# The last rows of a layer's second FFN in two parts of half their length, their output issued from two DMA queues

## The chip, the cores and the metric

The kernel is one program on all 8 cores of one Trainium2 chip. The metric is device time in microseconds (us), taken from the slowest core. Most executions agree within 0.3%; some fall in a slower state, in which the cores of one die or of both run at a lower granted clock. Those executions (one of before with 1,452 us, for example) are left out of every ratio and reading here; where a run had one, it still counts in the median that is quoted.

Some cores matter more than others. The program has two variants: even cores (0, 2, 4, 6) and odd cores (1, 3, 5, 7) cut their rows differently. Before the change the even cores are about 4 to 5 us slower than their odd neighbours, so they set the time.

Most of what follows happens in the last 35 us. Since this stretch begins some microseconds earlier or later from core to core and from run to run, I give times in this tail as **+x**: us after the start of the last eviction of a 512-column tile by VectorE. That instruction comes just before the part of the program that the change touches, and lies at 1,286 to 1,291 us on the even cores. The page of a profile and the views of a core have times from the start of the core's span instead.

## The reference, cut to what matters

One layer of a streaming encoder: half-step FFN, mixing by attention and convolution, second half-step FFN, final normalisation.

```python
def rmsnorm(x, g):
    x32 = x.astype(jnp.float32)
    r = x32 * lax.rsqrt(jnp.mean(x32 * x32, axis=-1, keepdims=True) + EPS)
    return (r * g.astype(jnp.float32)).astype(x.dtype)

def swiglu(h, w_gate, w_up, w_down):
    return (jax.nn.silu(h @ w_gate) * (h @ w_up)) @ w_down

# ... first FFN, attention, convolution ...
        x = x + 0.5 * swiglu(rmsnorm(x, ffn2_norm[l]), ffn2_gate[l], ffn2_up[l], ffn2_down[l])
    return rmsnorm(x, final_norm)          # (cut)
```

The input has 4 x 4096 rows of 1024 features; `D_FF` is 2816. So each core has about 2,048 rows, which it works through in two groups.

## The kernel before

Data lie transposed: features on the partitions, in 8 tiles of 128 features (`kc`), rows along the free axis. The second group of an even core is a block of 512 rows and a block of 512 rows whose last pass is done in two parts of 256; an odd core ends with blocks of 512, 384 and 256 rows.

```python
PLANS = ((((512, False), (384, False), (256, False)),
          ((512, False), (512, False, (256, 256)))),       # even cores: two groups
         (((512, True), (512, False), (256, False)),
          ((512, False), (384, False), (256, False))))     # odd cores
```

In the last pass of the second FFN (`fi == 1`, `hf == 1`), TensorE makes one tile of 128 features of one part at a time; VectorE evicts it from PSUM (the memory that TensorE writes to) and adds it to `xres`; ScalarE squares it, GpSimd sums the squares.

```python
fine = blocks if gi == 0 else blocks[:-1] + g.parts[blocks[-1]]
order = [(dg, s, dm2) for s in fine for dg in range(4) for dm2 in range(2)]
# ...
for dg, s, dm2 in order:
    b = fb_take()                                   # a PSUM bank, of four
    for fl in range(nf):
        mm(b, 0, wv[:, fl, dm2 * 128:(dm2 + 1) * 128], AT[:, fl, c0:c0 + n], n, ...)
    rk, xi = ... (keys("x", g, dm, s), xo)
    dve(... out=xo, in0=bk, scalar=0.5, in1=xi ..., n, (("ps", b),) + rk, (xk,))     # L1048
    square(stats[s], g, dm, s)                      # ScalarE: square; GpSimd: add
    if dm == 7:
        S.add(0, norm_fin(stats[s], g, s, 3))       # a task, started when its inputs are there
```

`norm_fin` sums over the partitions by matmul, makes 1/rms with Ln and Exp on ScalarE, then normalises the 8 tiles on VectorE and issues the output. The last part goes out in pieces of 2 tiles, everything else in one piece of 8:

```python
    for kc in range(8):
        xk, xin = ... (keys("x", g, kc, s), xsl(g, kc, s))
        dve(... out=dst, in0=xin, scalar=gcol, in1=rt ..., xk + (("rstd", rr), "cs"), (wk,))   # L823
        if idx == 3:
            w = 2 if gi == 1 and s == g.fine[-1] else 8
            if kc % w == w - 1:
                # ... dst, src: tiles i*w to (i+1)*w of the part
                P.dma("sp", lambda h, dst=dst, src=src: h.dma_start(out=dst, in_=src), ...)    # L835
```

Who waits for whom is worked out from names ("keys") of the data. A part reads with its own key **and the key of its whole block**, and a write waits for every reader of any key that overlaps:

```python
def keys(kind, g, kc, s):
    r = g.par[s]
    return tuple((kind, g.gi, kc, x) for x in ([s, r] if r != s else ...))

def _toks(self, e, reads, writes):
    # ...
    for k in writes:
        for k2 in self.overlap.get(k, ()):
            # ...
            for t in self.readers.get(k2, {}).values():   # waits for readers of overlapping keys
                if t[2] != e or e != "pe":
                    yield t
```

So ScalarE's square of a tile of the last rows is put down as a reader of that tile of the whole block. When VectorE later normalises the same tile of the *first* rows of the block, it waits for this square, though they touch different columns.

The softmax here doesn't subtract the row's maximum and nothing guards it: scores larger than these inputs give would overflow.

## Time and profile before

| | before |
|---|---|
| time, median of 3 runs | 1325.45 us (1325.04 to 1452.33, the last slow) |
| spans of the even cores | 1321.5 to 1323.3 us |
| spans of the odd cores | 1317.3 to 1318.3 us |
| TensorE busy on core 6 | 98% |
| even cores: last matmul of the last pass | +17.9 |
| VectorE's last instruction | +25.8 |
| last landing of output | +30.2 to +30.9 |
| end of the span | +33.9 to +34.9 |

From the page (core 6, the slowest): busy times, and the shares of the chain of waits that ended last.

```profile
PE 1292.1 (98%) x8666; PEld 740.4 (56%) x8666; DVE 487.1 (37%) x899; ACT 407.0 (31%) x727; POOL 229.0 (17%) x266
...
PE 92%; DVE 3%; DMA 2%; issue 1%; ACT 1%; SPq 0%; DVEq 0%; POOL 0%; ACTq 0%; POOLq 0%
```

TensorE (PE) is busy all the time, up to the tail. A change of the tail alone can win or lose only microseconds of 1,325.

Busy time by stretches of core 6, for TensorE (its matmuls, then its weight loads), VectorE, ScalarE and GpSimd; the last two columns are the share of the core's 16 DMA engines that is busy, and what they move in GB/s.

```profile
1300.00:1304.00 4.00, 4.00 (x39) 3.47 (x38) 4.00 (x9) 1.83 (x5) 1.36 (x2) 1.00 0.00 0
1304.00:1308.00 4.00, 2.34 (x22) 1.86 (x19) 4.00 (x10) 1.58 (x4) 2.77 (x4) 1.00 0.47 197
1308.00:1312.00 4.00, 0.66 (x3) 0.29 (x3) 3.56 (x9) 1.22 (x3) 0.33 (x1) 0.76 0.89 361
1312.00:1316.00 4.00, 0.00 (x0) 0.00 (x0) 2.21 (x6) 0.00 (x0) 0.00 (x0) 0.50 1.04 344
1316.00:1320.00 4.00, 0.00 (x0) 0.00 (x0) 0.00 (x0) 0.00 (x0) 0.00 (x0) 0.50 0.45 153
```

And its issues of output in this time (KB each, us from issue to landing):

```profile
yout<-xres SPq DMA_DIRECT2D x1, 2048.0 KB, 7.1
yout<-xres SPq DMA_DIRECT2D x1, 1024.0 KB, 6.3
yout<-xres SPq DMA_DIRECT2D x4, 256.0 KB, 4.9
```

2 MB of the first block of 512 rows are issued at +17.1, 1 MB of the first 256 rows at +22.15, four pieces of 256 KB from +23.5 on. From 1308 to nearly 1318 the DMA engines are full or nearly so (0.89 up to 1312, 1.04 after it; a share over 1 comes from how the view counts packets and means full): the output is what ends last.

### The profile page before, as it was taken

Reading aid. Unit: us, or ns where it says so; the run is one execution under the profiler, and the core shown is the slowest. Engines: PE = TensorE matmul, PEld = TensorE weight load, DVE = VectorE, ACT = ScalarE, POOL = GpSimd, SP = SyncE. Lnnn points to the kernel's source line nnn. Section 1 sums busy time; section 2 is a strip of 40 time slices with the busy share of each in tenths; the row PEclk is TensorE's granted clock in tenths of the full one; section 3 lists DMA queues with packets and bytes.
Section 4 is the critical chain, followed back from the end, with each engine's and each line's share of the span. In section 5 each row is a group of like instructions: output and inputs, shape, how many; then the busy total and the mean of one; then the engine's idle time right before and its main releaser. Section 6 shows DMA issues by size and latency. Waiting matters only on the chain.

```text
span 1323.3 us, 23324 instructions; the slowest of 8 cores (1317.3 to 1323.3 us)
## 1 busy us (share of the span) xinstructions
PE 1292.1 (98%) x8666; PEld 740.4 (56%) x8666; DVE 487.1 (37%) x899; ACT 407.0 (31%) x727; POOL 229.0 (17%) x266
## 2 busy tenths in 40 slices
PE   7999999999999999999999999999999999999995
PEld 3655655566665666665564444446566664444444
DVE  4522222263745522222266222125455362222125
ACT  3411011242666421001236110114338661101123
POOL 2263000341003320000161000014120220000022
PEclk9999999999999999999999999999999999999998
DMA  8795226244930753243445844342784125433503
GB/s 187 164 217 116 49 47 120 42 127 142 193 70 2 188 91 72 53 76 53 73 52 101 218 80 82 66 76 49 171 208 103 34 39 111 75 65 64 112 0 130
DMA packets 33923, 129.55 MB, mean 98 GB/s; under 512 B 2832, under 2 KB 13200, under 8 KB 26896
## 3 DMA queue, kind: packets, MB, share of 16 engines
q0 software_dynamic: 18752, 97.33, 38.9%
q1 hardware_dynamic: 15056, 30.68, 6.8%
q8 instruction: 73, 1.20, 0.4%
q14 instruction: 42, 0.34, 0.1%
HBM read 193.54 MB, written 18.68 MB: 160 GB/s over the span
## 4 chain that ended last, share of the span: by engine, by line
PE 92%; DVE 3%; DMA 2%; issue 1%; ACT 1%; SPq 0%; DVEq 0%; POOL 0%; ACTq 0%; POOLq 0%
PE psA L561 53%; PE ps L561 39%; DVE hT L823 1%; DMA gscr_1<-dreg 1%; DMA ring<-wgu 1%; DVE xres L1048 1%; DVE xres L823 0%; DMA dreg<-gscr_1 0%; ACT L569 0%; DMA xres<-xin 0%; ACT rstd L574 0%; SPq L1673 0%; DVE xres L1556 0%; ACT pb L574 0%; POOL ssb L771 0%
## 5 line engine op out<-in xcount | busy, mean ns | idle before, releaser
L561 PE MATMUL psA<-hT,ring 128*128 128x512 bf16 (+2 forms) x3792 | 691.4, 344 | 1.7 <-DVE dreg L1139 1.0
L561 PEld LDWEIGHTS psA<-hT,ring 128*128 128x128 bf16 x3792 | 370.6, 98 | 316.1 <-issue 3.6
L574 ACT ACTIVATE dreg<-psA 128x512 f32<-128x512 f32 (+3 forms) x279 | 162.3, 587 | 688.1 <-PE psA L561 678.6
L561 PE MATMUL ps<-at,ring 128*128 128x512 bf16 (+2 forms) x1920 | 326.6, 332 | 0.0
L1014 DVE TENSOR_TENSOR at<-psA,dreg 128x512 bf16<-128x512 f32 (+2 forms) x213 | 130.1, 612 | 450.7 <-PE psA L561 427.3
L561 PEld LDWEIGHTS ps<-at,ring 128*128 128x128 bf16 x1920 | 187.6, 98 | 137.2
L1048 DVE SCALAR_TENSOR_TENSOR xres<-ps,xres 128x512 f32<-128x512 f32 (+2 forms) x160 | 88.5, 556 | 168.0 <-PE ps L561 168.0
L766 POOL TENSOR_TENSOR ssum<-ssum,sq 128x512 f32<-128x512 f32 (+2 forms) x102 | 103.2, 1012 | 169.4 <-ACT sq L574 165.6
L668 POOL DMA_DIRECT2D ring<-wgu x47 | 25.6, 546 | 522.9 <-PE ps L561 261.0
L561 PE MATMUL ps<-dreg,ring 128*128 128x256 bf16 (+4 forms) x704 | 85.7, 274 | 2.1 <-DMA dreg<-gscr_1 1.5
L574 ACT ACTIVATE sq<-xres 128x256 bf16<-128x256 f32 (+2 forms) x108 | 55.3, 519 | 99.8 <-DVE xres L1048 66.7
L823 DVE SCALAR_TENSOR_TENSOR hT<-xres,cs_sb,rstd 128x256 bf16<-128x256 f32 (+2 forms) x120 | 70.4, 644 | 12.4 <-ACT rstd L574 12.4
L561 PEld LDWEIGHTS ps<-dreg,ring 128*128 128x128 bf16 x704 | 55.2, 98 | 23.1 <-issue 4.4
L561 PE MATMUL ps<-hT,ring 128*128 128x512 bf16 (+2 forms) x352 | 63.4, 336 | 0.0
L561 PEld LDWEIGHTS ps<-hT,ring 128*128 128x128 bf16 x352 | 33.6, 98 | 25.5 <-issue 0.4
L569 ACT ACT_TABLE_LOAD x36 | 46.2, 1283 | 0.6
L574 ACT ACTIVATE pb<-psA 128x1024 bf16<-128x1024 f32 (+2 forms) x42 | 37.7, 915 | 8.1 <-PE psA L561 7.9
L1556 DVE TENSOR_TENSOR xres<-ps,xres 128x256 f32<-128x256 f32 (+2 forms) x48 | 24.9, 531 | 37.2 <-PE ps L561 37.1
L1576 POOL TENSOR_TENSOR dreg<-pb 128x2560 bf16<-128x2560 bf16 x8 | 35.8, 4502 | 0.7 <-DMA cwscr<-dreg 0.7
L668 POOL DMA_DIRECT2D ring<-wdA x16 | 8.6, 537 | 135.7 <-PE psA L561 135.3
L561 PE MATMUL ps<-at,hT 128*128 128x512 bf16 x136 | 30.8, 379 | 0.0
L561 PE MATMUL psA<-cb_sb 64*128 64x64 bf16 (+3 forms) x456 | 27.8, 223 | 0.0
(93 smaller groups left out, 588.5 us busy)
## 6 DMA issues: line engine op xcount, KB each, us to landing
ring<-wgu POOLq DMA_DIRECT2D x41, 1024.0 KB, 8.4
ring<-wdA POOLq DMA_DIRECT2D x16, 768.0 KB, 8.6
ring<-wdB POOLq DMA_DIRECT2D x16, 640.0 KB, 7.9
ring<-cwscr POOLq DMA_DIRECT2D x16, 640.0 KB, 9.7
cwscr<-dreg SPq DMA_DIRECT2D x8, 640.0 KB, 6.1
ring<-wab POOLq DMA_DIRECT2D x8, 512.0 KB, 8.2
ring<-wout POOLq DMA_DIRECT2D x4, 1024.0 KB, 14.7
dreg<-xin SPq DMA_DIRECT2D x2, 2048.0 KB, 21.9
```

Of the source, the lines that this page charges most:

```text
L561: P.op("pe", lambda h: h.matmul(o, lhsT=lhsT, rhs=rhs, start=start, stop=stop, skip_group_check=True), (max(n / 2400.0 + 0.0025, 0.03) if ...
L569: P.op("act", lambda h: h.activation(out=cs[0:1, CS_N + i:CS_N + i + 1], in_=onesS[0:1, 0:1], func=func), 1.5, ("cb1",), ())
L574: P.op("act", lambda h: h.activation(out=out, in_=in_, func=func, **kw), 0.12 + n / 1200.0 + (0.09 * sum(isinstance(v, bass.AP) for v in k ...
L668: P.dma("pool", lambda h, dst=dst, src=src: h.dma_start(out=dst, in_=src), wtok(p, i), (256 if p.reads else 512) * w, reads=p.reads, after ...
L766: pool(lambda h: h.tensor_tensor(out=ss, in0=ss, in1=sqt, op=ALU.add), n, (sk, ("sq", i)), (sk,))
L823: dve(lambda h, dst=dst, xin=xin, gcol=gcol: h.scalar_tensor_tensor(out=dst, in0=xin, scalar=gcol, in1=rt, op0=ALU.mult, op1=ALU.mult), n, ...
L1014: dve(lambda h: h.tensor_tensor(out=at, in0=ub, in1=tt, op=ALU.mult), n, (("ps", bU), ("tmpF", ti)), (("AT", gi, fl, s),))
L1048: dve(lambda h, xo=xo, xi=xi, bk=bk: h.scalar_tensor_tensor(out=xo, in0=bk, scalar=0.5, in1=xi, op0=ALU.mult, op1=ALU.add), n, (("ps", b), ...
L1556: dve(lambda h, xo=xo, bk=bk: h.tensor_tensor(out=xo, in0=bk, in1=xo, op=ALU.add), n, (("ps", b),) + rk, (("x", gi, dm, s),))
L1576: P.op("pool", lambda h, o_=o_, i0=i0: h.tensor_tensor(out=o_, in0=i0, in1=i1, op=ALU.mult), 4.5, ("cmp", "ic", "cb"), (("cwb", i % 2),))
```

## The change

The intent: after the last matmul there remains a serial chain for the last rows (eviction, square, sum over features, Ln, Exp, normalise, output). With 128 rows in it instead of 256 it should be shorter. The last pass of the second group takes its last part as two halves (`g.last`); the last half goes out in two pieces of 4 tiles, the second of them issued by ScalarE (`"act"`) rather than SyncE (`"sp"`). The other three stages keep the old parts.

```diff
+        self.last, self.of = self.fine[:], {}
+        if gi:
+            p = self.last.pop()
+            for i in range(2):
+                f, n = len(self.n), self.n[p] // 2
+                ...
+                self.par[f], self.of[f] = self.par[p], p
+                self.last.append(f)
 ...
             def keys(kind, g, kc, s):
                 r = g.par[s]
+                if s in g.of:
+                    return tuple((kind, g.gi, kc, x) for x in dict.fromkeys((s, g.of[s], r)))
 ...
-                        w = 2 if gi == 1 and s == g.fine[-1] else 8
+                        w = 4 if gi == 1 and s == g.last[-1] else 8
 ...
-                            P.dma("sp", lambda h, dst=dst, src=src: h.dma_start(out=dst, in_=src),
+                            P.dma("act" if w == 4 and i else "sp", lambda h, dst=dst, src=src: h.dma_start(out=dst, in_=src),
 ...
-                        fine = blocks if gi == 0 else blocks[:-1] + g.parts[blocks[-1]]
+                        fine = blocks if gi == 0 else blocks[:-1] + (g.parts[blocks[-1]] if fi == 0 else [
+                            x for x in g.last if g.par[x] == blocks[-1]])
```

More of the change, by code (lines that the diff above doesn't have):

```diff
@@ L278, in __init__ @@
         self.fine = [f for i in self.main for f in self.parts[i]]
+        self.last, self.of = self.fine[:], {}
[3 more added lines that the diff above has]
+                f, n = len(self.n), self.n[p] // 2
+                self.n.append(n)
+                self.halo.append(False)
+                self.off.append(self.off[p] + i * n)
+                self.par[f], self.of[f] = self.par[p], p
+                self.last.append(f)
         self.M = self.T - self.H
@@ L422, in make @@
                         P.reg(("k", gi, j, s), "at", 2 * (MMAX * j + m0), 2 * (MMAX * j + m0 + n))
-                for s in g.fine:
+                for s in g.fine + list(g.of):
                     m0, n, w = g.off[s] - g.H, g.n[s], g.n[g.par[s]]
@@ L430, in make @@
                             P.reg(("h", gi, kc, s), "h%d" % kc, c0, c0 + n)
+                    if s in g.of:
+                        continue
                     for j in range(4):
@@ L700, in keys @@
                 r = g.par[s]
+                if s in g.of:
+                    return tuple((kind, g.gi, kc, x) for x in dict.fromkeys((s, g.of[s], r)))
                 return tuple((kind, g.gi, kc, x) for x in ([s, r] if r != s else [s] + [f for f in g.parts[s] if f != s]))
@@ L1779, in _unpack @@
         g = Group(i, blocks)
-        for n in (g.n[s] for s in g.fine):
+        for n in (g.n[s] for s in g.last):
             out.append(yo[:, 8 * o0:8 * (o0 + n)].reshape(128, 8, n).transpose(2, 1, 0).reshape(n, D)[_order(n)])
```

## The prediction

> **What bounds the kernel.** The page of the slowest core (6) gives TensorE 98% of 1323.3 us, and the chain of waits is 92% PE. So nothing before the last pass can change; the change only touches the tail. The even cores decide: 1321.5 to 1323.3 us against 1317.3 to 1318.3 for the odd ones (list of cores).
>
> **The tail of core 6 (timeline and DMA packets).** The last rows' 80 matmuls of 256 columns end at 1306.3. From 1297.8 to 1310.5 VectorE has almost no gap: it evicts PSUM (0.33 us apart at 256 columns) and normalises the block of 512 (about 0.8 us per piece) and the first 256 rows (0.40 us per piece). So the last eviction starts only at 1308.5, 2.2 us after its matmuls. Square, sum, Ln and Exp follow until 1310.9, then eight pieces of 0.40 us until 1314.2. The output of the first 256 rows is issued at 1310.6; from its first packet, 1311.6, to about 1318 the DMA engines are at a share of 1.0, moving 2,048 packets of 1 KB at 49 ns each over 16 engines. SP's issues for the last rows take up to 1.44 us instead of 0.37, and the last landing is at 1319.3. Then PE's closing branch takes 3.6 us on even cores only.
>
> **What the change does, costed from the trace.**
> - PE: 160 matmuls of 128 columns for 80 of 256. Start to start is 109 ns at 256 and 56 ns at 128 columns (conv matmuls, which also load weights each time): +0.2 us, plus one more set of three summing matmuls. [...]
> - VectorE: evictions at 512, 384 and 256 columns give an estimate of 0.20 us apart at 128. 16 of those replace 8 of 0.33: +0.6 us. Normalising 16 pieces of an estimated 0.26 replaces 8 of 0.40: +1.0 us in all, but only 2.1 instead of 3.2 us of it comes after the last Exp.
> - The last serial chain (eviction, square, sum, Ln, Exp) is about 0.4 us shorter.
> - DMA: the last 1 MB becomes 2,048 packets of 512 B. This trace has 512-byte packets at 27 to 29 ns, so 3.5 us instead of 3.1: +0.4 us.
> - Issue: ScalarE issues the last half, so SP's slow issues no longer delay it. But the DMA engines were saturated. [...] share 1.0 here agrees that the engines, not the issuing, limit.
>
> **On the critical path.** VectorE is full until about 1310.5, so the shorter chain after the last matmul mostly doesn't show: I expect its end at about 1315 (was 1314.2). The 256 rows' output is issued no earlier (1310.5 to 1311.3), and after it the same 2 MB has to drain, 0.4 us slower. Last landing about 1319.8 (was 1319.3); odd cores up to 1 us later, hidden. Net +0.3 us, between -2.5 and +3.
>
> **Predicted:** 1325.8 us, range 1322.5 to 1328.5. Faster by over 2%: 0.01; within 2%: 0.97; slower: 0.02.
>
> **Right or wrong by:** matmuls of 128 columns 56 ns apart; 512-byte packets about 28 ns; the output of the first 256 rows issued within 0.7 us of 1310.6 from the same point; DMA share about 1.0 until the end; last VectorE piece near 1315; last landing near 1319.8.
>
> **What would make it wrong:** the new program order lets VectorE finish the first 256 rows earlier, so that the DMA drains sooner (up to 2 us gained); PSUM banks, refilled twice as fast, stall PE behind VectorE (1 to 2 us lost); the second queue costs set-up; two of three runs in the slow state.

Two estimates give no source. For 0.26 us per piece, the trace of before (core 6) has instructions of 0.74 us at 512 columns and 0.47 at 256, so 128 columns less take about 0.13 off the 0.40. For the 0.4 us by which the last chain is to be shorter, none is given.

## More of the kernel before

The timeline of VectorE (DVE) on core 2: start, us that the group takes, line, operation, shapes, count, and in brackets idle time before it and what ended that.

```profile
1303.74 0.74 DVE L1048 SCALAR_TENSOR_TENSOR xres<-ps,xres 128x256 f32<-128x256 f32 x2
1304.41 0.87 DVE L823 SCALAR_TENSOR_TENSOR xres<-xres,cs_sb,rstd 128x256 f32<-128x256 f32 x2
1305.20 0.41 DVE L1048 SCALAR_TENSOR_TENSOR xres<-ps,xres 128x256 f32<-128x256 f32 x1
1305.53 1.43 DVE L823 SCALAR_TENSOR_TENSOR xres<-xres,cs_sb,rstd 128x256 f32<-128x256 f32 x2
1306.88 0.41 DVE L1048 SCALAR_TENSOR_TENSOR xres<-ps,xres 128x256 f32<-128x256 f32 x1
1307.21 1.66 DVE L823 SCALAR_TENSOR_TENSOR xres<-xres,cs_sb,rstd 128x256 f32<-128x256 f32 x4
1309.41 3.26 DVE L823 SCALAR_TENSOR_TENSOR xres<-xres,cs_sb,rstd 128x256 f32<-128x256 f32 x8 [0.54 <-ACT rstd L574]
```

L1048 evicts a tile of the last 256 rows, L823 normalises. There is no bracket before the last line: VectorE is full, mixing evictions of the last rows with the normalising of the first 256. Only the last rows' own chain (square, sum, Ln, Exp) leaves a gap, of 0.54 us.

## The result, and the profile after

Ratios are computed as the mean time of one kernel's fast runs over the mean of the other's in the same rounds, so they are not quite the ratio of the medians that I quote.

| | before | after |
|---|---|---|
| time, median of 4 runs | 1325.30 us (1325.04 to 1452.33, one of them slow) | 1330.14 us (1329.67 to 1331.48) |
| ratio of fast runs | | 1.0039, interval 1.0019 to 1.0059 |
| spans of the even cores | 1321.5 to 1323.3 us | 1328.4 to 1330.0 us |
| spans of the odd cores | 1317.3 to 1318.3 us | 1318.7 to 1321.1 us |
| even cores: last matmul of the last pass | +17.9 | +21.1 |
| output of the first 256 rows issued | +22.15 | +24.6 |
| VectorE's last instruction | +25.8 | +28.7 |
| last landing | +30.2 to +30.9 | +34.7 to +35.5 |
| end of the span | +33.9 to +34.9 | +39.5 to +40.8 |

The kernel is 0.4% slower. That is "the same" by the 2% rule, but 4.8 us is a real difference, and outside of the predicted range. The even cores lose more than the odd ones.

From the page after (core 0): busy times, the new queue, the chain of waits.

```profile
PE 1294.3 (97%) x8758; PEld 741.9 (56%) x8758; DVE 490.3 (37%) x915; ACT 408.6 (31%) x737; POOL 230.3 (17%) x271
...
q10 hardware_dynamic: 528, 0.26, 0.1%
...
PE 89%; DMA 4%; DVE 3%; issue 1%; ACT 1%; POOL 0%; SPq 0%; DVEq 0%; ACTq 0%; POOLq 0%
```

TensorE has 2.2 us more busy time and VectorE 3.2 us (each page is of its slowest core, 0 here and 6 before), and neither says where in the span the 4.8 us lie. (The larger DMA share of the chain lies in the load of the input at its start, which the change doesn't touch.) The tail says more. VectorE on core 2, from the same view as before:

```profile
1304.61 0.87 DVE L1064 SCALAR_TENSOR_TENSOR xres<-ps,xres 128x128 f32<-128x128 f32 x4
1305.81 1.05 DVE L838 SCALAR_TENSOR_TENSOR xres<-xres,cs_sb,rstd 128x256 f32<-128x256 f32 x2 [0.32 <-ACT ssum L587]
1306.78 0.47 DVE L1064 SCALAR_TENSOR_TENSOR xres<-ps,xres 128x128 f32<-128x128 f32 x2
1307.63 1.37 DVE L838 SCALAR_TENSOR_TENSOR xres<-xres,cs_sb,rstd 128x256 f32<-128x256 f32 x2 [0.37 <-ACT sq L587]
...
1309.77 1.13 DVE L838 SCALAR_TENSOR_TENSOR xres<-xres,cs_sb,rstd 128x256 f32<-128x256 f32 x2 [0.37 <-ACT sq L587]
...
1311.62 5.08 DVE L838 SCALAR_TENSOR_TENSOR xres<-xres,cs_sb,rstd 128x256 f32<-128x256 f32 x18 [0.32 <-ACT ssb L587]
```

Four brackets are new. VectorE, full before, stands four times for a *square* of ScalarE (`sq`, `ssum` and `ssb` hold squares) before it normalises tiles of the first 256 rows. It does not need those squares: they are of the last rows. ScalarE in its turn waits for VectorE to evict. The groups of instructions of this time (busy us, mean ns of one, idle us before and who ended it) and the waits of TensorE show the sums on core 2.

```profile
L838 DVE SCALAR_TENSOR_TENSOR xres<-xres,cs_sb,rstd 128x256 f32<-128x256 f32 x8 | 4.4, 594 | 1.4 <-ACT sq L587 0.7 <-ACT ssum L587 0.3 <-ACT ssb L587 0.3
```

```profile
PE ps L574 <- DVE xres L1064: 2.1, 4, 0.8
...
ACT ssb L587 <- DVE xres L1064: 2.6, 2, 1.3
```

TensorE waits 2.1 us for PSUM that VectorE evicts late. In before, TensorE didn't wait for VectorE at all here.

The DMA engines by stretches on core 6, and its last two issues:

```profile
1308.00:1312.00 4.00, 2.85 (x39) 2.34 (x36) 3.30 (x8) 1.50 (x8) 1.98 (x4) 1.00 0.78 328
1312.00:1316.00 4.00, 0.55 (x3) 0.19 (x2) 3.81 (x14) 0.86 (x4) 0.00 (x0) 0.85 0.50 163
1316.00:1320.00 4.00, 0.00 (x0) 0.00 (x0) 1.27 (x5) 0.00 (x0) 0.00 (x0) 0.50 1.01 301
```

```profile
yout<-xres SPq DMA_DIRECT2D x1, 256.0 KB, 5.4
yout<-xres ACTq DMA_DIRECT2D x1, 256.0 KB, 6.7
```

The share falls to 0.50 in the stretch from 1312 to 1316, where it was 1.04. The engines have drained the first block's output and wait for the next. And the last issue, on ScalarE's queue, itself takes long (ScalarE's timeline, core 6; the second number is how long the issue took):

```profile
1317.35 4.75 ACTq L850 DMA_DIRECT2D yout<-xres  x1
```

On the four even cores it takes 4.15, 3.97, 4.23 and 4.75 us, on the odd ones 0.42 to 0.43.

### The profile page after: what moved, and what is told of

It is laid out like the page before. It is cut to its first block, busy times and chain, and to the rows that moved or that the text cites. A ratio compares the mean times of both kernels' runs of the same rounds, so it can differ in the third digit from the quotient of the medians.

```text
span 1330.0 us, 23608 instructions; the slowest of 8 cores (1318.7 to 1330.0 us)
## 1 busy us (share of the span) xinstructions
PE 1294.3 (97%) x8758; PEld 741.9 (56%) x8758; DVE 490.3 (37%) x915; ACT 408.6 (31%) x737; POOL 230.3 (17%) x271
## 4 chain that ended last, share of the span: by engine, by line
PE 89%; DMA 4%; DVE 3%; issue 1%; ACT 1%; POOL 0%; SPq 0%; DVEq 0%; ACTq 0%; POOLq 0%
PE psA L574 51%; PE ps L574 38%; DMA xres<-xin 2%; DVE hT L838 1%; DMA gscr_0<-dreg 1%; DMA gscr_1<-dreg 1%; DVE xres L1064 0%; DVE xres L838 0%; ACT L582 0%; DMA dreg<-gscr_1 0%; POOL ring L681 0%; SPq L1689 0%; ACT rstd L587 0%; DVE xres L1572 0%; ACT dreg L587 0%
## 5 line engine op out<-in xcount | busy, mean ns | idle before, releaser
L574 PE MATMUL ps<-at,ring 128*128 128x512 bf16 (+3 forms) x2000 | 327.4, 325 | 2.0 <-DVE xres L1064 2.0
L1064 DVE SCALAR_TENSOR_TENSOR xres<-ps,xres 128x512 f32<-128x512 f32 (+3 forms) x168 | 88.9, 536 | 167.5 <-PE ps L574 167.5
L781 POOL TENSOR_TENSOR ssum<-ssum,sq 128x512 f32<-128x512 f32 (+3 forms) x106 | 104.1, 983 | 172.1 <-ACT sq L587 167.6
L587 ACT ACTIVATE sq<-xres 128x512 bf16<-128x512 f32 (+3 forms) x113 | 56.0, 504 | 100.2 <-DVE xres L1064 64.8
L838 DVE SCALAR_TENSOR_TENSOR xres<-xres,cs_sb,rstd 128x512 f32<-128x512 f32 (+3 forms) x56 | 28.0, 565 | 1.4 <-ACT sq L587 0.7
```

The lines of the kernel that those rows point to most:

```text
L574: P.op("pe", lambda h: h.matmul(o, lhsT=lhsT, rhs=rhs, start=start, stop=stop, skip_group_check=True), (max(n / 2400.0 + 0.0025, 0.03) if ...
L587: P.op("act", lambda h: h.activation(out=out, in_=in_, func=func, **kw), 0.12 + n / 1200.0 + (0.09 * sum(isinstance(v, bass.AP) for v in k ...
L781: pool(lambda h: h.tensor_tensor(out=ss, in0=ss, in1=sqt, op=ALU.add), n, (sk, ("sq", i)), (sk,))
L838: dve(lambda h, dst=dst, xin=xin, gcol=gcol: h.scalar_tensor_tensor(out=dst, in0=xin, scalar=gcol, in1=rt, op0=ALU.mult, op1=ALU.mult), n, ...
L1064: dve(lambda h, xo=xo, xi=xi, bk=bk: h.scalar_tensor_tensor(out=xo, in0=bk, scalar=0.5, in1=xi, op0=ALU.mult, op1=ALU.add), n, (("ps", b), ...
```

## The experiments

Two theories stand after the traces. The first: the second queue's issue is slow, and the last piece lands late for it. The second: the waits through the shared key of the block hold VectorE up. Rivals were that the four PSUM banks hold TensorE up, that the smaller packets of the output (512 B) are the cost, and that halving itself is. Where a recorded expectation gives letters to theories, what it says a theory expects tells which one it is. All kernels gave the reference's result.

### e1: the last piece on SyncE's queue

```diff
-  P.dma("act" if w == 4 and i else "sp", ...
+  P.dma("sp", ...
```

> The changed kernel with its very last output piece issued by SP instead of ScalarE; nothing else changed. Theory A (two costs: on even cores ScalarE takes 4.0 to 4.75 us to issue that piece, and VectorE is held back by waits on the other rows' squares): the last two pieces land within 1 us of each other, the last landing comes 1.5 to 2.0 us earlier after the same point, odd cores unchanged, time about 1328.4 us. Rival B (the loss is VectorE's extra work, PSUM and smaller packets; ScalarE's long issue only fills time in which the DMA engines are busy anyway): 0 to 0.5 us, about 1330 us.

Measured: 1328.41 us against 1325.11 for before, ratio 1.0028 (1.0011 to 1.0045). VectorE ends at +28.7 as in after; the last landing is at +33.3 to +34.1 instead of +34.7 to +35.5. By core it comes 0.8 to 2.1 us earlier, 1.3 us on average (expected 1.5 to 2.0), and the last two pieces land 0.7 to 2.1 us apart, not all within 1 us. So ScalarE's slow issue costs about 1.3 us of the 4.4 by which the landing had moved, and the greater part of the loss has another cause.

### e2: no shared key in the last pass; ScalarE still issues

A part still waits for whoever wrote the block, but is no longer put down as a reader of the whole block.

```diff
     for k in reads:
-        t = self.lastw.get(k)
+        t = self.lastw.get(k[1] if k[0] == "~" else k)
 ...
     for k in reads:
-        self.readers.setdefault(k, {})[tok[2]] = tok
+        if k[0] != "~":
+            self.readers.setdefault(k, {})[tok[2]] = tok
 ...
+def wkeys(g, kc, s):                    # used by the last pass's evictions, squares and normalising
+    ks = keys("x", g, kc, s)
+    return ks[:1] + tuple(("~", k) for k in ks[1:])
```

> The changed kernel, where in the last pass a read through the key of the whole block still waits for the block's last writer, but is no longer recorded as a reader of the whole block, so normalising rows 0 to 255 no longer waits for the squares of the last 128 rows. ScalarE still issues the last piece. Theory A: VectorE no longer waits for ScalarE in the last pass (it waited 4 times, 0.32 to 0.37 us each, plus the slots it lost), matmuls end 1 to 2 us earlier and VectorE ends 1.5 to 3 us earlier after the same point; time about 1327.5 us. Rival C (VectorE's plain work and the four PSUM banks, refilled twice as fast, set the pace): VectorE's end moves by less than 0.7 us, time within 0.7 us of the changed kernel.

Measured: two fast runs, 1325.34 and 1328.19 us, and two slow. The profiled run is one of the fast ones. VectorE waits for no square any more and ends at +26.35 (after: +28.72); the last landing is at +31.9 to +32.2, about 3 us earlier. The second theory holds, for the larger part of the loss. ScalarE's issue still takes 3.45 to 3.86 us. One expectation missed: TensorE's last matmul came at +20.97, not 1 to 2 us earlier than +21.06. TensorE's order of work, and its waits for PSUM, are thus not explained by the shared key.

### e3: both

> Both edits together: no recorded reads through the block's key, and all output issued by SP. Theory A: the two gains add, 3 to 5 us off the changed kernel, 1325 to 1327 us, level with the kernel before within 1 us. Rivals B and C: less than 1.5 us off, above 1328.5 us.

Measured: 1324.77 us against 1325.11, ratio 0.9997 (0.9981 to 1.0014). The whole loss is gone: last landing at +29.9 to +31.0 against +30.2 to +30.9 before. VectorE on core 2:

```profile
1306.82 0.87 DVE L847 SCALAR_TENSOR_TENSOR xres<-xres,cs_sb,rstd 128x256 f32<-128x256 f32 x2
1307.61 0.28 DVE L1075 SCALAR_TENSOR_TENSOR xres<-ps,xres 128x128 f32<-128x128 f32 x1
1307.81 0.87 DVE L847 SCALAR_TENSOR_TENSOR xres<-xres,cs_sb,rstd 128x256 f32<-128x256 f32 x2
...
1310.18 4.56 DVE L847 SCALAR_TENSOR_TENSOR xres<-xres,cs_sb,rstd 128x128 f32<-128x128 f32 x16
```

The brackets are gone. The eight pieces of the first 256 rows take 3.5 us of busy time instead of 4.4 in after, and 1.4 us of idle time fall away: together 2.3 of the 2.4 us by which VectorE ends earlier. Halving alone, then, is neither a gain nor a loss that these runs can tell (the interval is 2.5 us below to 1.9 above): all 16 pieces of the last rows still come after the last eviction (4.56 us, where before had 8 pieces in 3.26 us), and VectorE ends 0.5 us later than before. e3 still has the 512-byte packets and the four banks, so those two rivals don't account for the loss either.

### e4: before, with half of its last pieces on ScalarE's queue

The first theory, alone, on the other kernel.

```diff
-  P.dma("sp", ...
+  P.dma("act" if w == 2 and i > 1 else "sp", ...
```

> The kernel before (rows in one part of 256, four output pieces), with the last two of its four pieces issued by ScalarE. Theory A: ScalarE's first issue takes about 4 us on even cores and about 0.43 us on odd ones here too, although the part is not halved; the second of its issues follows at about 0.4 us; last landing 0.3 to 1.5 us later than before, time about 1326.2 us. Rival B: ScalarE's issues take below 1.5 us and relieve SP, time 0.3 to 1 us below the kernel before.

Measured: 1325.66 us, ratio 1.0005 (0.9985 to 1.0025). ScalarE's two issues take 0.43 and 0.56 to 0.86 us on the even cores (0.38 and 0.89 on core 7), not 4. So an issue on ScalarE's queue isn't slow as such: the theory in that form fell. Nor does a second queue gain anything where the engines behind it are full (in before, a share of 1.04 from 1312 to 1316): the last landing stays at +30.2 to +30.8.

### e7: before, without the shared key

```diff
   (the edit of e2, on the kernel before)
```

> The kernel before with the edit of e2_no_false alone. VectorE of the kernel before showed no wait for ScalarE's squares in its last pass. Theory A (those waits come only with the halved part): VectorE's end (+25.8 us after the first eviction of the last block's first half) and last landing (+30.6) move by less than 0.4 us. Rival: the waits cost the kernel before too, and its landing comes 1 us or more earlier.

Measured: the fast run gave 1324.94 us (the other was slow). VectorE ends at +25.7 to +25.8, last landing +30.8 to +31.1: nothing comes earlier (the landing is 0.4 us later on average). The shared key was in before too, but its waits were over before VectorE came to them. Halving made them bite. The timelines above suggest why, though no run tests it: more tiles of the last rows are evicted and squared between two tiles of the first rows.

### e8 and e9: where in ScalarE's program the slow issue stands

Why 4 us in after and 0.4 in e4? Counted in the trace, the slow issues are ScalarE's instruction 1853 (after) and 1852 (e2), e4's first, a fast one, is instruction 1825. And 1.0 to 1.3 us before a slow issue ends, packets of 8 KB end on a queue that the page calls "instruction" (q14). The third theory (F): the place in ScalarE's program decides; my guess was that ScalarE waits there for those packets, while the DMA engines are full of output. To test the place, e8 moves after's issue beyond it by 24 waits that are already fulfilled, spread over ScalarE's program; e9 moves e4's issue onto it by 27.

```diff
+  it = P.E["act"].items
+  first = next(i for i, x in enumerate(it) if x[0] == "op" and x[2])
+  for j in range(24):                  # e9: 27, on the kernel of e4
+      it.insert(first + 1 + 21 * j, ("wait", "e_act", 1))
```

> The changed kernel with 24 waits on ScalarE that are already fulfilled, spread from its start, so that every later instruction of ScalarE stands 24 places further on; nothing else. Seen so far on even cores: the issue by ScalarE took 4.0 to 4.75 us as ScalarE's traced instruction 1853 and 3.5 to 3.9 us as 1852, but 0.43 us as 1825; each long one ends about 1.2 us after an 8 KB packet of queue 14. Theory F [...]: at place 1877 the issue takes about 0.45 us on even cores, the last landing comes about 1.3 us earlier after the same point, time about 1328.5 us as with SP alone. Rival G (ScalarE's issue waits because SP's 160 descriptors per engine are still queued): it stays at 3.5 us or more, 1330 us.

> The kernel before with the last two of four pieces on ScalarE, plus 27 fulfilled waits, so that ScalarE's first issue stands at place 1852 instead of 1825. Theory F: this issue takes 3 to 5 us on even cores, with a packet of queue 14 about 1.2 us before it ends, and the second one about 0.4 us. Rival G: 0.43 us as before the shift.

Measured, in ScalarE's timeline of core 6, e8 and then e9 (two issues in one row):

```profile
1317.48 0.43 ACTq L850 DMA_DIRECT2D yout<-xres  x1
```

```profile
1311.71 4.13 ACTq L835 DMA_DIRECT2D yout<-xres  x2
```

e8: all issues on even cores take 0.43 us, the last landing is at +33.2 to +33.9 as in e1, VectorE's end unchanged; 1330.14 us against 1326.25, ratio 1.003 (1.0014 to 1.0047). The expected 1328.5 us was missed, but these rounds ran on another chip, where before took 1326.25 us and not 1325.11, so I go by the ratio (e1: 1.0028) and by the trace. e9: the first of the two issues takes 3.61 to 3.77 us on the even cores, the second 0.38; landing +31.2 to +31.4; 1326.06 us in one run. So the place decides, in both directions, and rival G (the descriptors of SyncE that are still queued) falls. That the issue waits for the packets of the instruction queue is only argued, from their times in the traces:

```
kernel, core    packets on the instruction queue          slow issue ends
after, 0        1321.77 to 1322.24                        1323.40
after, 6        1319.96 to 1320.93                        1322.10
e9, 6           1313.75 to 1314.09                        1315.32
```

On all even cores of after, e2 and e9 the issue ends 1.0 to 1.3 us after the last of these packets, and takes 3.0 to 4.3 us over the usual 0.43. Most such packets cost ScalarE nothing: in after, core 6 has 38 of them between 36 and 1,318 us (the trace doesn't tell for which engine), and behind only one of them, at 37 us, did ScalarE stand idle for over 0.3 us. Nor is the place alone enough: in e8 the instructions now at places 1852 and 1853 pass without a wait above 0.11 us, at 1308.3 on core 6, although the DMA engines are full there too (a share of 1.25 from 1308 to 1309). That full DMA engines slow these packets is likewise only argued, from a share of 1.01 between 1316 and 1320 on core 6 of after, where the slow issue starts at 1317.35. Shown is that the place of the issue costs the time; why it does stays open.

### e10: eight PSUM banks (on e3)

```diff
+  if gi == fi == hf == 1:
+      mode["lru"] += [b for b in range(4) if b not in mode["lru"]]
```

> Both edits of e3_both, and the last pass may use all eight PSUM banks instead of four. Theory V (VectorE is full from the first normalisation to the end, so that matmuls wait for it and not the other way round): PE's waits for VectorE in the last pass (2.0 us on core 2) go, matmuls end 2 to 3 us earlier after the same point (about +18.3 instead of +21.0 us), but VectorE's end stays within 0.5 us of +26.3 and the last landing within 0.7 us of +30.0. Rival C (the banks set the pace): VectorE ends and the output lands 1.5 to 3 us earlier.

The waits of TensorE on core 2, e3 and then e10:

```profile
PE ps L575 <- DVE xres L1075: 2.0, 3, 0.8
PE ps L575 <- POOL ssb L793: 1.0, 1, 1.0
```

```profile
PE ps L575 <- POOL ssb L793: 1.5, 1, 1.5
```

TensorE no longer waits for VectorE; its last matmul comes at +19.2 instead of +21.0 (expected +18.3). But VectorE ends at +26.7, if anything later, and the last landing is at +30.8 to +31.9, later than the +29.3 to +30.7 expected (one run, 1327.88 us). So the banks did hold TensorE up, and freeing them gained nothing: VectorE sets the pace there, and TensorE now waits elsewhere.

### e12 and e13: the parts before the last in pieces of 4 tiles

What, then, holds the end in e3 and before alike? The output of earlier parts could start sooner if it went out in pieces. e12 is e3, e13 is before; the block of 512 rows is still one piece.

```diff
-  w = 4 if gi == 1 and s == g.last[-1] else 8                # e12, on e3
+  w = 4 if gi == 1 and s != g.main[0] else 8
-  w = 2 if gi == 1 and s == g.fine[-1] else 8                # e13, on before
+  w = 2 if gi == 1 and s == g.fine[-1] else 4 if gi == 1 and s != g.main[0] else 8
```

> Both edits of e3_both, and the output of the rows before the last parts (on even cores the first 256 rows of the last block) also written in two pieces of four tiles, the first as soon as it is normalised. The DMA engines were full from 0.9 us after that output's issue (+21.6 us after the first eviction of the last block) to the end (+29.6), so a first piece about 2 us earlier lets the rest drain earlier: last landing at about +29.0 instead of +30.0 on even cores, bounded by VectorE's end (+26.3, unchanged) and about 2.5 us from the last issue to landing. Time 0.5 to 1.5 us below the kernel before. Rival: the landing is set by VectorE's end and the issues after it alone, and stays within 0.3 us of +30.0.

> The kernel before (part of 256, four last pieces, SP alone) with only that same earlier piece. If what the halving was to win is a matter of when the output starts, this wins it without the halving: SP's long issues (1.2 to 1.44 us) fall below 0.8 us, VectorE's end stays at +25.8, the last landing moves from +30.6 to about +29.2 on even cores, time 0.7 to 1.5 us below the kernel before, level with e12_early_pieces. Rival: less than 0.3 us, because the last piece alone sets the end.

Measured: e12 1324.90 us, ratio 0.9997 (0.9983 to 1.0011) (of the 2.5 us that its expectation takes from the last issue to landing, the nearest figure is a later one, 2.4 us as the median of four pieces of 256 KB in e15); e13 1324.50, ratio 0.9995 (0.9981 to 1.0009). On even cores the last landing didn't move (e12: +29.9, +30.9 on core 0, where I had expected about +29; e13: +30.65). On even cores SyncE's issues in e13 still took up to 1.2 us, not below 0.8. On odd cores, which don't set the time, e13 landed 1.9 us earlier. The reason for the miss: the 2 MB of the block of 512 rows, issued at +17.1, occupy the DMA engines to about +22.9 (a mean share of 0.98 from 1305 to 1309.5 on core 6 of e13). The piece issued in between, at +20.2, moved its packets only from then on.

### e14 and e15: all outputs of the second group in pieces of 4 tiles

So the block of 512 rows must start earlier, too.

```diff
-  w = 2 if gi == 1 and s == g.fine[-1] else 8                # e14, on before
+  w = 2 if gi == 1 and s == g.fine[-1] else 4 if gi == 1 else 8
-  w = 4 if gi == 1 and s == g.last[-1] else 8                # e15, on e3
+  w = 4 if gi == 1 else 8
```

> The kernel before with the outputs of all earlier parts of the second group (the block of 512 rows too) written in two pieces of four tiles each; the last part of 256 in four pieces, SP alone. Reading e13_before_pieces: on even cores the first 256 rows' piece was issued at +20.2 us but its packets moved only from +22.9, when the 2 MB of the block of 512 rows, issued at +17.1, had nearly drained; the engines are occupied from +18 to +30.3. Theory D (this drain, from the block of 512 rows on, sets the even cores' end): half of that output issued at about +13 lets everything after it move up, and the last landing goes from +30.6 to +28.7 to +29.3, now bounded by VectorE's end at +25.8 and its last piece; time about 1.5 us below the kernel before. Rival (the last pieces alone set it): +30.3 to +30.7 as in e13.

> Both edits of e3_both and all outputs of the second group in pieces of four tiles (block of 512 rows, first 256 rows, both last parts of 128). Theory D: last landing on even cores from +30.0 to +29.0 to +29.4, bounded by VectorE's end, which the halving leaves at +26.3 against +25.8; so this is level with or up to 0.5 us behind e14_before_all_pieces, and 1 to 1.5 us below the kernel before. Rival: with VectorE no longer delayed and the drain out of the way, the halving wins 0.5 us or more over e14.

e14: **1322.78 us against 1325.51, ratio 0.9978 (0.9965 to 0.9991)**: 0.2% faster than before, the same by the 2% rule but clear of the noise, while after was 0.4% slower. The first half of the block's output is issued at +12.9 instead of +17.1. The last landing moves to +28.7 to +29.4, although VectorE ends where it did, at +25.7. Its stretches on core 6 begin to move output where before had a DMA share of 0.00:

```profile
1300.00:1304.00 4.00, 4.00 (x39) 3.49 (x37) 4.00 (x7) 1.82 (x5) 2.22 (x3) 1.00 0.64 262
...
1312.00:1316.00 4.00, 0.00 (x0) 0.00 (x0) 0.84 (x3) 0.00 (x0) 0.00 (x0) 0.50 0.73 248
```

e15, the halves with the same pieces: 1325.06 us, ratio 0.9996 (0.9983 to 1.0009). Its last landing is at +28.7, as early as e14's, but its spans end at +34.2 to +34.9, e14's at +32.6 to +33.3. Something after the landing costs nearly 2 us.

### e16 and e17: what comes after the landing

Each core ends with a barrier of all engines (in before, core 6: semaphore instructions of all five between 1319.42 and 1319.61). In the trace, GpSimd's last instruction before it is a DRAIN, which begins with GpSimd's last operation and lasts 8.5 to 8.9 us. It ends 8.1 us after that operation, whenever that is:

```
core 0          DRAIN on GpSimd        last landing   PE's closing branch starts, takes
e14             1306.63 to 1315.41     1316.39        1316.78, 3.42
e15             1309.68 to 1318.45     1316.43        1318.78, 3.67
```

With halves, GpSimd's last addition comes later, and so does the DRAIN's end. The timelines of GpSimd (POOL) on core 0, e14 and then e15:

```profile
1306.66 0.67 POOL L771 TENSOR_TENSOR ssb<-ssum,sq 128x256 bf16<-128x256 f32 x1 [0.20 <-POOL ssum L766]
```

```profile
1309.70 0.65 POOL L793 TENSOR_TENSOR ssb<-ssum,sq 128x128 bf16<-128x128 f32 x1 [0.27 <-PE ps L563]
```

To test it, e16 takes the late work off GpSimd (the last 128 rows' squares are summed by 8 matmuls), and e17 gives e14 a single tiny late instruction on GpSimd.

```diff
+  if st.get("pe"):                                            # e16, on e15; last part only
+      o_, ok = ssum_t[:, r, :].bitcast(BF16)[:, 128 * k:128 * k + n], ("ssq", r, k)
+      act(o_, xin, AF.Square, n, xk, (ok,))
+      st.setdefault("rhs", []).append((ok, o_))               # each a matmul with ones
+      return
+  P.E["pool"].items.append(("wait", "e_act", P.E["act"].count))                        # e17, on e14
+  P.E["pool"].items.append(("op", lambda h: h.memset(sq_t[:, 0, 0:64], 0.0), False))
```

> e15_halves_all_pieces, where the squares of the very last 128 rows are summed by eight matmuls instead of five additions on GpSimd and three matmuls. Theory P (GpSimd's closing drain of about 8.7 us starts after its last addition and holds the end): GpSimd's last addition ends some 4 us earlier, its drain ends before the last landing, the closing follows the landing by 0.1 us instead of 2.0 us on even cores; time 1.5 to 2.5 us below e15, about 1322.8 us, level with e14_before_all_pieces. Rival: the closing still comes 2 us after the landing, time as e15 (1325).

> e14_before_all_pieces with one tiny GpSimd instruction (64 columns set to zero in a buffer no longer used) after ScalarE's last Exp, at about +22.5 us after the first eviction of the last block. Theory P: GpSimd's drain of about 8.7 us starts there and ends near +31.5, 2 to 3 us after the last landing (+28.7 to +29.4), and the even cores end 2 to 3 us later although nothing else changes. Rival: the drain starts at the end whenever it likes and the closing still follows the landing by 0.1 us.

e16: the DRAIN ends before the landing, the barrier follows 0.10 us after it, the last landing is at +28.45: 1323.29 us against 1325.83, ratio 0.9986 (0.9971 to 1.0001). That is 1.8 us below e15 by the medians and 1.3 by the ratios, which come from different rounds; in the tail the even cores end at +32.2 to +32.7 instead of +34.2 to +34.9. It is about level with e14, and no better. e17: the memset, in GpSimd's timeline of core 0,

```profile
1313.65 0.15 POOL L1642 MEMSET sq<- 128x64 bf16 x1 [2.65 <-ACT rstd L574]
```

takes 0.15 us, but the DRAIN behind it takes 8.23 us, and the even cores close 1.4 to 1.8 us after the landing instead of 0.10. They end at +34.4 to +34.9 rather than +32.6 to +33.3 (the time of this one run, 1328.08 us against 1325.83, is higher by more than that, but a single run can't be told apart from scatter; the tail is what I read). An instruction of 0.15 us, on an engine that is busy for 17% of the span, thus cost about 1.7 us of the tail (2 to 3 expected). In e3 the close follows the landing by 0.84 to 0.89 us instead of 0.10 on three of four even cores, and in e12 by 0.69 to 0.94; in before, after and e14 the DRAIN delays nothing.

## Why the prediction was wrong

The right parts first.

- *What bounds the kernel.* Only the tail moved, and the even cores decided, as predicted.
- *DMA.* 512-byte packets took 27 to 28 ns (predicted about 28).
- *Matmul cost.* 128-column matmuls follow each other in 56 ns where they aren't held up.
- *VectorE's own costs.* Evictions 0.20 us apart at 128 columns, normalising 0.26 to 0.28 us. In e3, free of the waits, VectorE ends 0.5 us later than before; I had predicted about 0.8.

The steps that failed:

1. **"VectorE is full until about 1310.5"**, carried over from before, and **"the 256 rows' output is issued no earlier (1310.5 to 1311.3)"**. It was issued 2.5 us *later* (+24.6 for +22.15), and VectorE ended 2.9 us later, not 0.8. The halves interleave with the first 256 rows so that the shared key's waits bite, four times on core 2, with 1.4 us idle and 0.9 us more busy time for the same eight pieces. Removing the record of these readers (e2) moved the landing by about 3 us. I had costed instructions by length and number, and not asked what they wait for in the new order. The code showed it: the key of the whole block is in `keys`.
2. **"ScalarE issues the last half, so SP's slow issues no longer delay it."** I listed set-up of the second queue as a risk, without a size. SP's slow issues weren't the limit (e4: ratio 1.0005); ScalarE's issue became one, because of its place in ScalarE's program (moved away from it in e8, it took 0.43 us): 3.97 to 4.75 us, worth 1.3 to 1.4 us of landing on average (e1, e8). I had a DMA share of 1.0 in the trace, and should have drawn the conclusion that the second queue had nothing to win.
3. **TensorE "+0.2 us".** Its last matmul came 3.2 us later. The PSUM banks that I listed under "what would make it wrong" did stall it (2.1 us waiting for VectorE), but this was off the critical path: e10 took these waits away and nothing ended earlier.
4. **"DMA share about 1.0 until the end."** It fell to 0.50 from 1312 to 1316 on core 6, because the output of the first 256 rows came late. That was the predicted sign to look for, and it showed the failed step.

The sum: last landings of the even cores are at +30.6 on average before and +35.0 after, 4.4 us later. e2 gives back 3.0 us of this and e1 1.3 us; with both (e3, +30.2 on average) nothing is left. The gain hoped for from a shorter last chain doesn't exist, since VectorE is full up to the last rows and since the DMA engines are full or nearly so from shortly after the issue of the block of 512 rows (e12 to e14). What remained open: in after, the closing branch of TensorE (COMPARE_BRANCH in the trace) took 4.3 to 5.3 us on the even cores, 3.3 to 3.8 us before; in e1 5.1 us on one core and about 3.4 on three. This adds some 1.2 us on top of the landing in the profiled run of after. The traces show where it goes: 1.0 to 1.5 us after the branch starts, a packet of 16 KB moves on another queue that the page calls "instruction" (q8), and the branch ends 1.35 to 1.43 us after the last such packet. The packet took 1.0 to 1.2 us in before and 1.9 to 2.8 us in after (on two cores there it was the second of a pair). No experiment says why it took longer.

## What to carry to other kernels

When you cut a piece of work finer, ask first which waits its new order will meet: a dependence recorded for a whole block can be free in one order and cost microseconds in another, as e7 against e2 shows (without it the landing came 0.4 us later in e7, about 3 us earlier in e2). At the end of a kernel, look at when the DMA engines begin to be full rather than at the last serial chain: starting the large output 4 us sooner (e14, ratio 0.9978) gained what halving the last rows could not. And look at what the slowest engine to close does after its last instruction, since even a memset of 0.15 us moved the end by about 1.7 us (e17).

## What else the traces show

- VectorE's closing DRAIN lasted 1.8 to 2.8 us in before and after, but only because VectorE was still working: it ended 0.05 us after VectorE's last operation, where GpSimd's ends 8.1 us after GpSimd's.
- Packets of 512 B took 27 to 28 ns, of 1 KB 46 to 49 ns and of 16 KB 615 to 624 ns. By stretches of the trace the 16 engines moved about 280 to 310 GB/s in packets of 512 B and about 340 of 1 KB; for 16 KB, 16 engines at 615 to 624 ns a packet give an estimate of 420 to 426. So the rate still grew above 512 B here.
- The closing branch of TensorE took 3.3 to 5.3 us on the even cores in before and after; on the odd ones the traces have none, and their spans end 0.3 us after the landing.
